# Two-layer hybrid encoder: mLSTM convolution without zero columns, and full-height rows of the running maximum

## Chip, cores and metric

The kernel runs on one core of one Trainium2 chip. The metric is the device time of one execution in microseconds; of a kernel several executions are timed and the median is taken. Lower is better.

## What is computed

The reference is an encoder of two layers over 256 tokens of width 1024, all in float32. A layer normalises `x`, multiplies it by one wide matrix, and hands the parts to four branches: A, a bidirectional mLSTM of 4 heads; B, grouped-query attention with rotary position codes; C, neighbourhood attention; D, differential attention. Each branch's result is projected up and gated, their sum goes through an output projection, and a SwiGLU feed-forward follows. The change touches branch A, of which this is the core:

```python
def centred_dwconv(x, w):
    k = w.shape[0]
    p = k // 2
    s = x.shape[1]
    xp = jnp.pad(x, ((0, 0), (p, p), (0, 0)))
    return sum(xp[:, j:j + s, :] * w[j] for j in range(k))

qk = jax.nn.silu(centred_dwconv(jnp.concatenate([q, k], axis=-1), conv_w))
...
dmat = jnp.where(lower, bt[..., :, None] - bt[..., None, :] + it[..., None, :], -jnp.inf)
inter = bt + m[..., None]
mt = jnp.maximum(inter, dmat.max(-1))
```

The convolution has three taps over tokens, with a zero beyond each end. `mt` is a running maximum per token, head and direction, by which the exponentials are stabilised.

## The kernel before

The weights stream from HBM in halves of 128x1024. ScalarE rounds each half (`whi`), VectorE takes the rest (`wlo`), and TensorE forms every dense product in three passes over these parts into PSUM banks `pd`. Units of weights follow each other in the order of `PLAN` (L38): per layer the inputs of D, B and A, then gates and up-projections between the other branches' inputs, then the output projection and the feed-forward.

The branches' own work is put between the dense products. Each piece is a generator that issues some instructions and yields. Between two runs of dense products (six matmuls as a rule) the program has a slot (`slot`, L296). There `step` (L281) lets each piece advance once if the planner believes that what the piece issued last is through. For this, `Meter` (L140) adds up an estimated cost of each instruction per engine, and all instructions pass through it, which is why nearly every row of the profile shows line 166. On POOL it reckons 0.3 + 0.165 n us for a power of n elements and 0.1 + 0.0021 n us for anything else (L152, 153). A piece's due time is the latest end, on VectorE, ScalarE and POOL, of the engines on which it has just issued something, plus 0.2 us; a step that issued nothing on these three is due at once:

```python
before = [e.until for e in (V, A, G)]
try:
    next(t)
    ready[t] = max([e.until + LAT for e, u in zip((V, A, G), before) if e.until != u] or [0.0])
```

The order so made is fixed at build time; on the chip each engine works through its own queue in that order and waits for semaphores.

`a_head` (L603 to 702) is the piece for one mLSTM head. It takes three tiles `w` (`xp`, `cv`, `th`), transposes the head's q and k on TensorE into a `pa` bank (L613), and has POOL write zeros into the first and last column of each half of `xp` (L617, 618). Next step: ScalarE copies the bank into the columns between (L620) and writes the centre tap's product into `cv` (L625). Next: VectorE adds the outer taps, four instructions of 256 columns (L628 to 630). Then ScalarE's tanh (L632), VectorE's product with 1 + tanh (L634), and on TensorE the scores, `cv` by `cv` in float32 (L640 to 642, `pa<-w` in the profile), and the running maximum (L643 to 647): a matmul by a column of `identr`, a unit matrix, broadcasts one row of `mrow` over 128 partitions, for two directions and the two parts of the number. `mrow` (L213) and `identr` (L201) have 36 partitions; `a_gates` (L518) writes `mrow` once per layer. Two heads are in flight at a time (`fly`).

Beside head 2 and 3, `b_main` (L951) does the rotary codes of branch B on POOL: a power of 20 elements (L974), then for each token tile the products of the keys (`ktok`) and of the queries (`k` tiles of the profile, 512 columns). POOL executes in order.

Of the kernel before, what the change touches and what calls it, by code (L numbers as in the profile page):

```python
# [11 lines left out]
F32 = mybir.dt.float32  # L12
F32R = mybir.dt.float32r
# [6 lines left out]
S = 256  # L20
# [6 lines left out]
# scheduling: how far the engines may be queued ahead of the tensor engine, how early a piece may advance, what a  # L27
# result takes to reach another engine
FILL, TOL, LAT = 2.5, 0.1, 0.2

# column offsets inside w_in
# [10 lines left out]
# offsets inside the per-layer parameter tile  # L42
# [5 lines left out]
# per-feature columns: norm1 gain, norm2 gain, convolution taps  # L48
# [3 lines left out]
# offsets inside the constant tile  # L52
# [4 lines left out]
def unit_order():  # L57
    """Weight units of one layer in the order in which the tensor engine uses them."""
    o = []
    for n in PLAN:  # L60
        if n == "bkv":
            o += [("bkv", 0, 0), ("bkv", 1, 0)]
        elif n[0] == "u":
            o += [("up", n[1], int(n[2]))]
        else:
            o += [("in", n, 0), ("in", n, 1)]
    for kh in (0, 1):
        for c in (0, 1):
            o += [("wo", kh, c)]
    for j in range(NFB):  # L70
        o += [("gu", j, 0), ("gu", j, 1)]
        if 1 <= j < NFB - 1:
            o += [("dn", j - 1, 0)]
    o += [("dn", NFB - 2, 0), ("dn", NFB - 1, 0)]
    return o
# [5 lines left out]
class Res:  # L81
    """Free list over persistent tiles."""
# [20 lines left out]
class Track:  # L103
    """Estimates of when the regions of tiles are written and read by what was emitted so far; it only orders the program."""
# [15 lines left out]
    def after(self, who, reads, writes):  # L120
        """Earliest start of an instruction of `who` by the regions it touches."""
        t = 0.0
        for aps, wr in ((reads, False), (writes, True)):
            for ap in aps:
                name, lo, hi = self.region(ap)
                for l, h, w, e, end in self.acc.get(name, ()):
                    if l < hi and lo < h and (w or wr or name[0:2] in ("pa", "pd")) and e is not who:
                        t = max(t, end + self.HOP)
        return t
# [10 lines left out]
class Meter:  # L140
    """Passes instructions on to an engine and keeps an estimate of when it is through with them."""
# [29 lines left out]
def trunk(ctx: ExitStack, tc, x_in, wts, par, parc, cst, dist, t2w, fg, out):  # L171
# [29 lines left out]
    identr = sb("identr", [36, 128], F32R)  # L201
# [11 lines left out]
    mrow = sb("mrow", [36, 2, S], F32R)  # L213
# [15 lines left out]
    with tc.manual_schedule():  # L229
# [24 lines left out]
        def halves(h):  # L254
            """The first piece is split in two steps, so that the tensor engine can begin after one of them."""
            return (slice(0, 512), slice(512, 1024)) if h == 0 else (slice(0, width(h)),)
# [24 lines left out]
        def step(lst, forced):  # L281
            """Each piece advances once what it issued last is through, as far as the engines have room."""
            for t in list(lst):
                if not forced:
                    if lst is tasks and max(V.until, A.until) > T.until + FILL:
                        return
                    if ready.get(t, 0.0) > T.until + TOL:
                        continue
# [4 lines that stand above are left out]
                except StopIteration:  # L293
                    lst.remove(t)

        def slot(forced=False):  # L296
            """Everything that goes between two runs of dense products; forced: between no products, for what they need."""
# [6 lines left out]
            # at the start the activations come before the weights that follow  # L304
# [13 lines left out]
        def after(eng, t, d=LAT):  # L318
            """Starts a piece once the engine is through."""
            ready[t] = eng.until + d  # L320
            urgent.append(t)

        def later(f, d=1):
            """Runs f after d more slots."""
            pending.append((d, f))

        def until(cond):
            """Advances everything else until the condition holds."""
# [12 lines left out]
        class Unit:  # L341
            """One weight unit [128, 2048], kept as two halves."""
# [28 lines left out]
        def blk512(units, lhs, nkt, done):  # L371
            """[256 tokens, 512] product over the units; the last unit runs one token tile after the other."""
# [60 lines left out]
        G.memset(iz, 0.0)  # L433
        G.memset(va[:, :, :, 128:129], 1.0)

        def tables():
            yield
            yield
            A.activation(identr, ident[0:36, :], AF.Copy)
# [9 lines left out]
        def boundary_chunk(t, c, gcol, st):  # L449
            """Transposes columns [512c, 512c+512) of token tile t into xT and adds to the sums of squares."""  # L450
# [37 lines left out]
        def yt_ok(b):  # L488
            """A branch takes a tile only if one is left for each branch that comes before it."""
# [28 lines left out]
        def a_gates(res):  # L518
            """Gate pre-activations -> a and threshold per token (columns), M as rows (split)."""
# [48 lines left out]
            # w1 rows: [a | B]; w2, w0 rows: zero-padded buffers of the running maximum  # L568
# [16 lines left out]
            A.activation(mrow[:, 0, :], m, AF.Copy)  # L585
            yield
            A.activation(br, br, AF.Exp, scale=-1.0)
            sub_lo(mrow[:, 1, :], m, mrow[:, 0, :])
# [14 lines left out]
        def a_head(B, h, pc):  # L603
            """Short convolution of q and k, then both directions of one head."""
# [11 lines left out]
            xv_ = xp[:, :516].rearrange("p (i n) -> p i n", i=2)  # L616
            G.memset(xv_[:, :, 0:1], 0.0)  # L617
            G.memset(xv_[:, :, 257:258], 0.0)
            yield
            A.activation(xv_[:, :, 1:257], p.rearrange("p (i n) -> p i n", i=2), AF.Copy)  # L620
# [7 lines left out]
            for i in (0, 1):  # L628
                V.scalar_tensor_tensor(cs_[i], xv_[:, i, 0:256], taps[i][0], cs_[i], op0=ALU.mult, op1=ALU.add)
                V.scalar_tensor_tensor(cs_[i], xv_[:, i, 2:258], taps[i][2], cs_[i], op0=ALU.mult, op1=ALU.add)  # L630
# [12 lines left out]
            for d in (0, 1):  # L643
                r = 32 * d + h
                for n in (0, 1):
                    T.matmul(pM[:, d * 256:(d + 1) * 256], identr[0:36, r:r + 1].to_broadcast([36, 128]),
# [90 lines left out]
        def soft_item(B, i, kind):  # L737
            """Two score rows (two heads, or the two components of a head) against all queries."""
            # the scores of D come divided by the head's slope, a power of two: the distances are then added as they are
# [107 lines left out]
        def soft_tail(B, i, c, e):  # L847
            """Normalised weights of one head [2 x 128 queries, 256 keys] -> transposed output rows."""
# [16 lines left out]
            # columns [high part | low part] of the values against the high part of the weights, then the high part  # L865
            # of the values against the low part of the weights
# [28 lines left out]
        def pair_src(B):  # L895
            """Blocks [q 2 pairs | k 2 pairs] in token layout; a block is free after its second pair."""
# [54 lines left out]
        def b_main(B):  # L951
# [12 lines left out]
            # sums of squares per head: 8 query heads then 2 key heads, per token tile  # L964
# [76 lines left out]
        def warm(n):  # L1041
            """Keeps the tensor engine's clock up until the first operands are there."""
# [20 lines left out]
        for l in range(L):  # L1063
# [7 lines left out]
            def tok_evac(B, key, tl=None, halves=False, early=False):  # L1071
# [9 lines left out]
                def done(t, p):  # L1081
                    if halves:
                        if B is Bd:
                            # queries of two heads, times 4 ** (head + 1) / 8
# [19 lines left out]
            def bkv_block():  # L1104
                """Keys and values of B and the gates of A."""
# [25 lines left out]
            def split_v(o, p, t):  # L1131
                """Scaled values, per head [high part | low part]."""
# [92 lines left out]
            # output projection  # L1225
# [28 lines left out]
            # feed-forward  # L1254
# [77 lines left out]
            def final_piece(t, o, n, p):  # L1332
                """Residual and final norm of columns [o, o + n); the last piece of a token tile sends it out."""
# [21 lines left out]
            def last_block():  # L1355
                """The last quarter in two narrow pieces, so that little is left to do after the last product."""
# [12 lines left out]
            # the first half waits longer for the last block's activations, the second ends one token tile after the other  # L1369
# [22 lines left out]
def _layout(inp):  # L1392
    """Host-side layout only: reordering, gathering by static indices, broadcasting of rows."""
    f = {k: np.asarray(v) for k, v in inp.items()}
    # rotary pairs of a head are brought next to each other: [row x1 | col x1 | row x2 | col x2]
# [54 lines left out]
    # neighbourhood bias: entry [p, slot, kc] of a query at column p%64 in row p//64 of its tile  # L1450
# [9 lines left out]
def _consts():  # L1460
    """Tables that depend on shapes alone."""
# [39 lines left out]
```

## Time and profile before

| | |
|---|---|
| runs of the kernel | 1111.65 to 1112.48 us, median 1112.28 us (3 runs) |
| profiled execution | span 1109.9 us from the first to the last instruction, 14766 instructions; the page lists no total beside the span |
| TensorE matmuls (PE) | busy 1086.8 us, 5272 instructions |
| VectorE (DVE) | busy 767.6 us |
| ScalarE (ACT) | busy 616.5 us |
| POOL | busy 156.8 us |
| mean granted clock of TensorE | 0.991 |
| DMA | 184.80 MB, mean 167 GB/s |

Times are in microseconds from the start of the span. A busy time tells how long an engine had an instruction in work; for TensorE, whose matmuls overlap, a busy time near the span doesn't mean that it runs at its peak. Idle time of an engine is put down to what released it. The granted clock is given as a share of 2.4 GHz, so 0.50 is 1.2 GHz. `out<-in` names tiles without their numbers: `w` stands for all of the eight general tiles, `pa` for the five PSUM banks of the pieces, `pd` for the three of the dense products.

### The profile page before, as it was taken

Reading aid. Unit: us, or ns where it says so; the run is one execution under the profiler, and the core shown is the slowest. Engines: PE = TensorE matmul, PEld = TensorE weight load, DVE = VectorE, ACT = ScalarE, POOL = GpSimd, SP = SyncE. Lnnn points to the kernel's source line nnn. Section 1 sums busy time; section 2 is a strip of 40 time slices with the busy share of each in tenths; the row PEclk is TensorE's granted clock in tenths of the full one; section 3 lists DMA queues with packets and bytes.
Section 4 is the critical chain, followed back from the end, with each engine's and each line's share of the span. In section 5 each row is a group of like instructions: output and inputs, shape, how many; then the busy total and the mean of one; then the engine's idle time right before and its main releaser. Section 6 shows DMA issues by size and latency. Waiting matters only on the chain.

```text
span 1109.9 us, 14766 instructions
## 1 busy us (share of the span) xinstructions
PE 1086.8 (98%) x5272; PEld 882.2 (79%) x5272; DVE 767.6 (69%) x1361; ACT 616.5 (56%) x1095; POOL 156.8 (14%) x145
## 2 busy tenths in 40 slices
PE   9999989999999999999999999999999999999997
PEld 7887867888888888888788887778888888888885
DVE  6689779889555755564576978798875666555554
ACT  7665547685444644444467656486853555444443
POOL 0001335054210000000000006152423000000000
PEclk9999989999999999999999999899999999999999
DMA  8444434445555555645544443344456445565551
GB/s 287 153 156 158 148 101 143 154 153 165 193 174 169 190 191 173 204 164 180 187 157 146 159 152 133 115 161 158 140 187 199 162 166 192 184 198 170 190 179 67
DMA packets 52329, 184.80 MB, mean 167 GB/s; under 512 B 6049, under 2 KB 6433, under 8 KB 52257
## 3 DMA queue, kind: packets, MB, share of 16 engines
q1 hardware_dynamic: 50112, 178.57, 48.3%
q10 hardware_dynamic: 2144, 5.31, 1.5%
q8 instruction: 41, 0.67, 0.3%
q14 instruction: 32, 0.25, 0.1%
HBM read 182.80 MB, written 1.05 MB: 166 GB/s over the span
## 4 chain that ended last, share of the span: by engine, by line
PE 77%; issue 13%; DVE 4%; POOL 3%; DMA 1%; ACT 1%; ACTq 0%; POOLq 0%; DVEq 0%
PE pd L166 55%; PE pa L166 22%; DVE sm L166 1%; DVE wlo L166 1%; DVE w L166 1%; DMA x<-in_x_dram 1%; POOL bsm L166 1%; POOL w L166 1%; POOL ktok L166 1%; DVE k L166 1%; DMA raw<-in_wts_dram 0%; POOL sm L166 0%; ACT w L166 0%; DVE rq L166 0%; ACT yt L166 0%
## 5 line engine op out<-in xcount | busy, mean ns | idle before, releaser
L166 PE MATMUL pd<-whi,xT 128*128 128x512 f32 (+1 forms) x1984 | 645.0, 396 | 0.0
L166 DVE TENSOR_TENSOR wlo<-raw,whi 128x1024 fp32r<-128x1024 f32 (+2 forms) x341 | 421.3, 1247 | 106.6 <-ACT whi L166 105.6
L166 PEld LDWEIGHTS pd<-whi,xT 128*128 128x128 f32 x1984 | 371.4, 188 | 86.7
L166 ACT ACTIVATE whi<-raw 128x1024 fp32r<-128x1024 f32 (+2 forms) x341 | 353.7, 1047 | 142.9 <-PE pd L166 91.3
L166 PE MATMUL pd<-wlo,xT 128*128 128x512 f32 (+1 forms) x992 | 387.5, 391 | 0.0
L166 PEld LDWEIGHTS pd<-wlo,xT 128*128 128x128 f32 x992 | 186.5, 188 | 39.4 <-DVE wlo L166 0.3
L166 PE MATMUL pa<-whi,yt 128*128 128x512 f32 x408 | 138.7, 402 | 1.4 <-ACT yt L166 1.4
L166 PEld LDWEIGHTS pa<-whi,yt 128*128 128x128 f32 x408 | 76.6, 188 | 19.7 <-ACT yt L166 1.8
L166 PE MATMUL pd<-whi,yt 128*128 128x512 f32 (+1 forms) x272 | 90.7, 402 | 0.0
L166 PE MATMUL pa<-wlo,yt 128*128 128x512 f32 x204 | 80.6, 395 | 0.0
L166 DVE SCALAR_TENSOR_TENSOR w<-w,pd 128x256 f32<-128x256 f32 x44 | 18.5, 421 | 88.3 <-ACT w L166 88.1
L166 POOL TENSOR_TENSOR st<-st,mhalf 128x2 f32<-128x2 f32 (+1 forms) x6 | 3.9, 656 | 521.6 <-DVE st L166 521.6
L166 ACT ACTIVATE k<-pd,st 128x512 f32<-128x512 f32 (+1 forms) x52 | 31.5, 623 | 56.0 <-PE pd L166 56.0
L166 PEld LDWEIGHTS pd<-whi,yt 128*128 128x128 f32 x272 | 52.4, 194 | 11.9 <-issue 0.4
L166 ACT ACTIVATE w<-pd,st 128x256 f32<-128x256 f32 (+1 forms) x48 | 23.7, 493 | 55.1 <-PE pd L166 52.7
L166 PE MATMUL pd<-wlo,yt 128*128 128x512 f32 (+1 forms) x136 | 54.2, 398 | 0.0
L166 ACT ACTIVATE yt<-pa 128x512 fp32r<-128x512 f32 x34 | 20.3, 598 | 56.2 <-PE pa L166 56.2
L166 PEld LDWEIGHTS pa<-wlo,yt 128*128 128x128 f32 x204 | 38.4, 188 | 8.0
L166 POOL TENSOR_TENSOR acc<-acc,k 128x512 f32<-128x512 f32 x16 | 33.0, 2061 | 80.2 <-DVE k L166 80.2
L166 POOL TENSOR_TENSOR w<-w,sm 128x512 f32<-128x512 f32 x32 | 39.4, 1254 | 21.9 <-DVE sm L166 21.9
L166 ACT ACTIVATE w<-pa 64x256 f32<-64x256 f32 (+3 forms) x66 | 26.7, 409 | 26.7 <-PE pa L166 12.7
L166 DVE TENSOR_TENSOR yt<-pa,yt 128x512 fp32r<-128x512 f32 x30 | 20.7, 689 | 29.1 <-ACT yt L166 29.1
(153 smaller groups left out, 1019.0 us busy)
## 6 DMA issues: line engine op xcount, KB each, us to landing
raw<-in_wts_dram SPq DMA_DIRECT2D x332, 512.0 KB, 3.7
t<-in_t2w_dram ACTq DMA_DIRECT2D x8, 384.0 KB, 3.3
raw<-in_wts_dram SPq DMA_DIRECT2D x8, 272.0 KB, 2.9
pt<-in_par_dram SPq DMA_DIRECT2D x1, 584.0 KB, 7.0
pt<-in_par_dram ACTq DMA_DIRECT2D x1, 584.0 KB, 3.6
out_dram<-k SPq DMA_DIRECT2D x2, 288.0 KB, 2.1
x<-in_x_dram ACTq DMA_DIRECT2D x1, 512.0 KB, 9.7
k<-in_fg_dram ACTq DMA_DIRECT2D x1, 512.0 KB, 3.5
```

The lines of the kernel that those rows point to most:

```text
L166: return f(out, *a, **k)
```

## The change

Three edits. The zero columns and their memsets go: `xp` holds 2 x 256 columns without a gap, and the outer taps leave out the column that would have read a zero. `mrow` and `identr` get 128 partitions, so that the broadcast matmuls contract over 128 rows; the rows beyond 36 of `mrow` are zeroed once at the start. Comments are taken out all over the file, which the program doesn't see and which is left out here.

```diff
-    identr = sb("identr", [36, 128], F32R)
+    identr = sb("identr", [128, 36], F32R)
...
-    mrow = sb("mrow", [36, 2, S], F32R)
+    mrow = sb("mrow", [128, 2, S], F32R)
...
         G.memset(iz, 0.0)
+        G.memset(mrow.bitcast(F32), 0.0)
...
-            A.activation(identr, ident[0:36, :], AF.Copy)
+            A.activation(identr, ident[:, 0:36], AF.Copy)
...
-            A.activation(mrow[:, 0, :], m, AF.Copy)
+            A.activation(mrow[0:36, 0, :], m, AF.Copy)
...
-            sub_lo(mrow[:, 1, :], m, mrow[:, 0, :])
+            sub_lo(mrow[0:36, 1, :], m, mrow[0:36, 0, :])
...
-            xv_ = xp[:, :516].rearrange("p (i n) -> p i n", i=2)
-            G.memset(xv_[:, :, 0:1], 0.0)
-            G.memset(xv_[:, :, 257:258], 0.0)
-            yield
-            A.activation(xv_[:, :, 1:257], p.rearrange("p (i n) -> p i n", i=2), AF.Copy)
+            xv_ = xp[:, :512].rearrange("p (i n) -> p i n", i=2)
+            yield
+            A.activation(xp[:, :512], p, AF.Copy)
...
             for i in (0, 1):
-                V.scalar_tensor_tensor(cs_[i], xv_[:, i, 0:256], taps[i][0], cs_[i], op0=ALU.mult, op1=ALU.add)
-                V.scalar_tensor_tensor(cs_[i], xv_[:, i, 2:258], taps[i][2], cs_[i], op0=ALU.mult, op1=ALU.add)
+                V.scalar_tensor_tensor(cs_[i][:, 1:256], xv_[:, i, 0:255], taps[i][0], cs_[i][:, 1:256],
+                                       op0=ALU.mult, op1=ALU.add)
+                V.scalar_tensor_tensor(cs_[i][:, 0:255], xv_[:, i, 1:256], taps[i][2], cs_[i][:, 0:255],
+                                       op0=ALU.mult, op1=ALU.add)
...
-                    T.matmul(pM[:, d * 256:(d + 1) * 256], identr[0:36, r:r + 1].to_broadcast([36, 128]),
+                    T.matmul(pM[:, d * 256:(d + 1) * 256], identr[:, r:r + 1].to_broadcast([128, 128]),
                              mrow[:, n, :], start=n == 0, stop=n == 1)
```

## Rows read from the trace of the kernel before

**Rows 1.** The page, part 1: busy us (share of the span) x instructions.

```profile
PE 1086.8 (98%) x5272; PEld 882.2 (79%) x5272; DVE 767.6 (69%) x1361; ACT 616.5 (56%) x1095; POOL 156.8 (14%) x145
```

**Rows 2.** Waits of TensorE: us in total, times, longest us.

```profile
PE pa L166 <- DVE w L166: 9.9, 2, 5.0
PE pa L166 <- DVE rq L166: 1.9, 2, 0.9
```

**Rows 3.** Windows: length, busy us (x instructions) of each engine, PEclk, DMA share, GB/s.

```profile
60.00:146.80 86.80, 84.56 (x413) 67.91 (x411) 74.02 (x169) 52.64 (x98) 21.85 (x29) 1.00 0.45 148
147.00:157.00 10.00, 7.47 (x18) 5.55 (x19) 7.71 (x18) 2.80 (x5) 1.85 (x2) 0.50 0.31 105
157.10:696.30 539.20, 532.79 (x2603) 432.54 (x2601) 375.81 (x658) 303.94 (x538) 77.54 (x67) 1.00 0.51 167
696.50:703.00 6.50, 6.50 (x16) 4.77 (x17) 4.23 (x12) 1.23 (x2) 0.00 (x0) 0.50 0.24 81
```

**Rows 4.** Timeline of TensorE, both layers: start us, us, what, idle before it.

```profile
149.53 2.07 PE L166 MATMUL pa<-w 128*128 128x256 f32 x4 [4.96 <-DVE w L166]
...
696.45 2.08 PE L166 MATMUL pa<-w 128*128 128x256 f32 x4 [4.95 <-DVE w L166]
```

**Rows 5.** Timeline of POOL, ScalarE and VectorE ahead of the first layer's wait.

```profile
128.64 4.44 POOL L166 TENSOR_TENSOR bsm<-bsm,mhalf 128x20 f32<-128x20 f32 x1 [22.15 <-DVE bsm L166]
...
139.23 0.14 POOL L166 MEMSET w<- 128x2 f32 x2
...
139.40 0.60 ACT L166 ACTIVATE w<-pa 128x512 f32<-128x512 f32 x1 [3.57 <-POOL w L166]
...
140.47 4.33 DVE L166 SCALAR_TENSOR_TENSOR w<-w,pc,w 128x256 f32<-128x256 f32 x4 [2.92 <-ACT w L166]
...
140.83 2.79 POOL L166 TENSOR_TENSOR k<-k,w 128x512 f32<-128x512 f32 x2
...
144.72 1.75 DVE L166 TENSOR_TENSOR wlo<-raw,whi 128x1024 fp32r<-128x1024 f32 x1
...
147.80 1.67 DVE L166 SCALAR_TENSOR_TENSOR w<-w,w 128x512 f32<-128x512 f32 x1
```

**Rows 6.** The same timeline, 134 to 138 us, TensorE, ScalarE and VectorE.

```profile
134.23 0.60 PE L166 MATMUL pa<-ident,acc 128*128 128x128 f32 x4
...
134.78 1.05 ACT L166 ACTIVATE whi<-raw 128x1024 fp32r<-128x1024 f32 x1
...
135.27 1.14 DVE L166 TENSOR_TENSOR w<-w,pa 128x256 f32<-128x256 f32 x4
...
136.33 1.21 DVE L166 TENSOR_TENSOR wlo<-raw,whi 128x1024 fp32r<-128x1024 f32 x1
```

**Rows 7.** The chain of waits: start us, us, what; one run of six dense matmuls.

```profile
165.27 1.40 PE pd L166 x6
```

**Rows 8.** Timeline: head 2's convolution, and POOL's products of `ktok`.

```profile
125.35 1.98 DVE L166 SCALAR_TENSOR_TENSOR w<-w,pc,w 128x256 f32<-128x256 f32 x4
...
136.11 1.62 POOL L166 TENSOR_TENSOR w<-ktok,w 128x64 f32<-128x64 f32 x2
```

**Rows 9.** Timeline of TensorE: the `mrow` block, and a block of full height.

```profile
132.06 0.73 PE L166 MATMUL pa<-mrow,identr 36*128 36x256 f32 x4
132.72 0.51 PE L166 MATMUL pd<-whi,xT 128*128 128x512 f32 x1
...
132.06 0.53 PEld L166 LDWEIGHTS pa<-mrow,identr 36*128 36x128 f32 x4 [0.33 <-issue]
...
189.21 0.63 PE L166 MATMUL pa<-re,vb 128*128 128x256 f32 x4
189.68 1.04 PE L166 MATMUL pa<-ident,k 128*128 128x128 f32 x8
```

**Rows 10.** Groups of POOL by form: busy us, mean ns, idle before.

```profile
L166 POOL MEMSET w<- 36x512 f32 x4 | 2.0, 519 | 67.2 <-ACT w L166 34.8 <-PE pd L166 32.5
```

**Rows 11.** Timeline of ScalarE: head 1's copy.

```profile
89.28 0.60 ACT L166 ACTIVATE w<-pa 128x512 f32<-128x512 f32 x1 [0.74 <-POOL w L166]
```

## The prediction

> **What bounds the kernel now.** I read the busy shares first. TensorE is busy for 1086.8 of 1109.9 us [rows 1], so only two things can shorten the program: less matmul time, or the few stretches in which TensorE stands still or runs slowly. The waits of TensorE name the stretches in which it stands: in the whole trace it waits 9.9 us for VectorE's `w` tiles, in 2 waits of up to 5.0 us, and little else [rows 2]. The windows show those in which it is slow: between 60 and 703 us the granted clock is 1.00 except in two stretches, 147 to 157 and 696.5 to 703 us, where it is 0.50, that is 1.2 instead of 2.4 GHz [rows 3]. The timeline shows that both belong together: TensorE idles 4.96 us before the `pa<-w` matmuls at 149.53 and 4.95 us before those at 696.45, and the slow clock covers each wait's end and what follows [rows 4]. It is the same place in both layers: the score matmul (L641) of head 3 of the mLSTM branch, with dense products queued behind it.
>
> Followed backwards [rows 5]: the matmul needs `cv`, finished by VectorE's 1.67 us instruction at 147.80 (L634); that needs the tanh (L632), that the convolution (4.33 us from 140.47, L628 to 630), and that ScalarE's copy at 139.40 (L620), which stood 3.57 us, by the trace for POOL's `w`. POOL's two memsets of zero columns (L617, 618) run at 139.23. They need nothing that late; they stand in POOL's queue behind the rotary work of branch B, which begins with a power of 4.44 us at 128.64 on which the planner reckons 0.3 + 0.165 x 20 = 3.6 us. So a write of two columns puts off a chain that TensorE waits for. From the timeline alone the copy could have run when the transposes (0.60 us from 134.23) were through, near 134.9; in ScalarE's queue a `whi` split stands there until 135.83 [rows 6].
>
> **The memsets (removed).** The stalls cost 4.96 + 4.95 = 9.9 us idle. At half clock TensorE was busy 7.47 us in one stretch and 6.50 us in the other [rows 3], which at full clock take half: 7.0 us lost. Together 16.9 us are to be had. How much of it comes back hangs on the new chain. Copy: without the memsets the first step of `a_head` writes on no engine but TensorE, so its `ready` is 0 and the copy is emitted at the next slot instead of after the planner's estimate for POOL. I take that as one slot (six dense matmuls, 1.40 us [rows 7]), which puts the copy ahead of that `whi`: copy and the two centre taps 134.9 to 136.3. Convolution: VectorE is then through its four products (1.14 us from 135.27), so it can start at 136.4, ahead of the `wlo` of 136.33 [rows 6]. Its length is open. Head 2's took 1.98 us while POOL was idle; head 3's 4.33 us, beside POOL's `k` products of 1.4 us each [rows 5, 8]. At 136.4 POOL does the small products of the `ktok` part, two in 1.62 us [rows 8]. Bounds 1.98 and 4.33 us; I take 3.2, the middle, since POOL is busy but with shorter work. Then VectorE makes that `wlo` (1.21 us [rows 6], beside POOL 1.75 [rows 5]) while ScalarE does the tanh, and then L634, 1.67 us beside POOL, less than half of that if the convolution's ratio holds for it. With 1.2 for each: 136.4 + 3.2 + 1.2 + 1.2 = 142.0; at the bounds 136.4 + 1.98 + 1.21 + 0.76 = 140.3 and 136.4 + 4.33 + 1.75 + 1.67 = 144.2.
>
> The Trainium skill (SBUF — State Buffer, section "SBUF: two separate sides") has a rule that speaks against this move: a VectorE instruction with two SBUF inputs and a POOL instruction that reads SBUF lock each other out for a whole instruction. The trace agrees in kind (1.98 against 4.33 us); by the rule each of the four instructions could lose one `ktok` product, some 2 us (an estimate), and end inside the bounds above.
>
> When does TensorE ask? It arrived at 149.53 - 4.96 = 144.57; every later step of the piece moves one slot up too, so now at about 143.2. Against 142.0 that is no wait, at the worst bound 1.0 us. An idle time of 0.9 us (the `rq` waits, rows 2) lies in the stretch from 157 to 696 us, whose clock is 1.00 [rows 3], so a rest of that size costs no clock. I put 0.5 us per layer, 1.0 in all, with 0 and 2.0 as ends.
>
> **Late next.** The stall let the other engines catch up; without it TensorE comes some 8 us (16.9 / 2) sooner to what follows. VectorE has the 2.92 us before the convolution, where it idled [rows 5], and the split weights due then come earlier than now. I add nothing beyond the 1.0 us.
>
> **The full-height rows.** Eight times (4 heads, 2 layers) four matmuls multiply 36 rows of `mrow` by a broadcast column. The block takes 132.72 - 132.06 = 0.66 us, and its first weight load waits 0.33 us of "issue", so it doesn't lie under the matmul before it [rows 9]. The nearest block of four full-height matmuls of 256 columns takes 189.68 - 189.21 = 0.47 us [rows 9]. Hence 0.19 us saved if the new block behaves like that row, and up to 0.33 more for the entry; 0 if the height means nothing. A loss I exclude: the columns streamed are the same. Between 0 and 0.52 us I take 0.25, nearer to 0.19 because the matmul before the block still streams during part of the 0.33: 8 x 0.25 = 2.0 us, ends 0 and 4.2.
>
> By the Trainium skill (TensorEngine Tiling (Array Packing), section "Key Properties") a change of tiling mode drains TensorE; the 0.33 us at the entry agree, and by that rule alone the sum would lose the whole of it, 8 x 0.52 = 4.2 us instead of 2.0 (an estimate).
>
> **The rest.** The outer taps are one column shorter of 256 (1 ns each) and the copy writes the same 512 columns: nothing. `identr` holds 36 columns instead of 128: one ScalarE instruction at the start, nothing. A memset of `mrow` is added, 128x512, against 0.52 us for a 36x512 one [rows 10]; POOL runs it in the first 2 us and has no other work until the first norm, and `mrow` is first read beyond 100 us: nothing; uncovered it would cost about that 0.5 us once. Head 1's copy also waits for POOL, 0.74 us [rows 11], without a wait of TensorE behind it (its matmul waits for the gates): nothing. It moves up by about two slots, and with it some 2 us of VectorE work; TensorE waits for VectorE nowhere near it (the two waits on `w` are head 3's), so nothing again. No DMA is added or moved. Comments are removed too.
>
> **Sum.** 1109.9 - 16.9 + 1.0 - 2.0 = 1092.0 us of span. The page gives no total of the profiled execution beside its span; the median of the runs, 1112.28, is 2.4 us above it, and I keep these 2.4: **1094.4 us**, 1.6% less. Own range: 1112.3 - 16.9 - 4.2 = 1091.2 to 1112.3 - 16.9 + 2.0 + 0 = 1097.4.
>
> **Rivals.**
>
> *A shorter wait that still drops the clock.* If the convolution and L634 keep their durations of now and VectorE's order lets nothing be gained but the 3.57 us of the copy, while TensorE asks one slot earlier, 4.96 - 3.57 + 1.40 = 2.8 us of idle time stay per layer. For it: POOL works on until 149 either way. The clock was still 1.00 up to 146.8 us, 2.2 us into the first wait [rows 3], and then fell, so the 7.0 us of slow clock stay: 1112.3 - 16.9 - 2.0 + 2 x 2.8 + 7.0 = 1106.0. Against it: VectorE stood idle for 2.92 us before the convolution, and the shift moves it out of the `k` products.
>
> *The wait is not the memsets'.* The copy's release could hang on the tile's former reader, so that it stays at 139.4, and only the height of the rows counts: 1110.3, or 1112.3 if that gives nothing. Against it: the copy starts 0.17 us after the memsets do.
>
> *Slower: asked for sooner, ready no sooner.* If POOL's port holds the convolution until the same 144.8 as now, wherever it starts, while the planner, which knows of no such hold, emits L641 one slot sooner, each stall grows by 1.40 us; the slow clock follows it. With nothing from the height, 1112.3 + 2.8 + 0.5 (the second stretch of slow clock grown to the first's, half of 7.47 - 6.50) = 1115.6. It decides from the point at which the convolution ends after 144.8; against it stands that 8.4 us pass from 136.4 to there, for work of 1.98.
>
> **How the numbers follow.** Forecast 0.73 (1091.2 to 1097.4), shorter wait 0.13 (1106.0), not the memsets' 0.08 (1110.3 to 1112.3), slower 0.06 (1115.6). The range takes in the first two: 1091 to 1106, 0.86 of the chance. A measurement of this kernel tells 0.2% (2.2 us, 1110.1 to 1114.5) from no change; so faster 0.86, same 0.08, slower 0.06.
>
> **What the changed profile would show.** Right: no `w<- 128x2` memset on POOL; TensorE's waits for VectorE's `w` down from 9.9 to under 2 us; granted clock 1.00 from 60 to 690 us; head 3's convolution some 3 to 4 us earlier relative to POOL's power; the `mrow` matmuls as 128*128, a block near 0.5 us, without the 0.33 us of "issue". Wrong: a wait over 2 us before a `pa<-w`, or a new one within the 30 us behind it (`wlo`, `rq`), with the clock at 0.50 after it; or the copy still waiting for POOL.

## The result and the profile after

The changed kernel takes 1093.42 us (median of 4 runs, 1091.94 to 1093.63), the kernel before on the same chip 1111.99 (4 runs, 1111.65 to 1112.48): 18.6 us or 1.7% less, ratio 0.9832 with an interval of 0.9818 to 0.9846. The forecast was 1094.4. The profiled execution took 1093.29 us, its span is 1091.5 us against 1109.9 before, so 1.8 us lie around it.

The page of the changed kernel, part 1:

```profile
PE 1077.9 (99%) x5272; PEld 879.6 (81%) x5272; DVE 765.2 (70%) x1361; ACT 616.8 (57%) x1095; POOL 156.6 (14%) x130
```

Beside [rows 1], POOL has 15 instructions fewer: 16 memsets gone (8 heads with 2 each), one of `mrow` added. All other engines issue as many as before. TensorE is busy 8.9 us less, though its 5272 matmuls are the same in number: it ran at half clock for less time, and 32 of them are of another height.

The waits of TensorE (us in total, times, longest us), to be read beside [rows 2]:

```profile
PE pa L166 <- DVE rq L166: 3.0, 2, 1.5
...
PE pa L166 <- DMA x<-in_x_dram: 1.0, 1, 1.0
```

The line for VectorE's `w`, 9.9 us before, is gone. The one for `rq` has grown from 1.9 to 3.0.

The timeline of the changed kernel, first layer, head 3 (start us, us, what, idle before it), beside [rows 5]:

```profile
126.36 4.46 POOL L166 TENSOR_TENSOR bsm<-bsm,mhalf 128x20 f32<-128x20 f32 x1 [20.40 <-DVE bsm L166]
...
132.09 0.58 ACT L166 ACTIVATE w<-pa 128x512 f32<-128x512 f32 x1
...
133.64 2.23 DVE L166 SCALAR_TENSOR_TENSOR w<-w,pc,w 128x255 f32<-128x255 f32 x4
...
133.96 1.02 POOL L166 TENSOR_TENSOR w<-ktok,w 128x64 f32<-128x64 f32 x2
...
135.79 1.48 DVE L166 TENSOR_TENSOR wlo<-raw,whi 128x1024 fp32r<-128x1024 f32 x1
...
137.19 0.88 DVE L166 SCALAR_TENSOR_TENSOR w<-w,w 128x512 f32<-128x512 f32 x1
...
140.05 1.02 PE L166 MATMUL pa<-w 128*128 128x256 f32 x4
```

The two traces are shifted against each other, so times are counted from the start of POOL's power. ScalarE's copy came at 10.8 us, now at 5.7, with no wait in its brackets; the convolution began at 11.8, now at 7.3; L634 ended at 20.8, now at 11.7. TensorE was ready for the scores at 15.9 (144.57) and stood until 20.9; now it takes them up at 13.7, when they have been there for 2.0 us (138.07 against 140.05).

The `mrow` block of head 2 in TensorE's timeline, changed kernel, beside [rows 9]:

```profile
128.53 1.02 PE L166 MATMUL pa<-w 128*128 128x256 f32 x4
129.21 0.83 PE L166 MATMUL pa<-mrow,identr 128*128 128x256 f32 x4
129.87 0.39 PE L166 MATMUL pd<-whi,xT 128*128 128x512 f32 x1
130.10 0.40 PE L166 MATMUL pd<-wlo,xT 128*128 128x512 f32 x1
...
129.18 0.64 PEld L166 LDWEIGHTS pa<-mrow,identr 128*128 128x128 f32 x4
```

The weight load no longer waits 0.33 us for "issue". The block itself takes 129.87 - 129.21 = 0.66 us, as long as with 36 rows; what is saved lies at its two ends. From the first score matmul to the second dense one it is 130.10 - 128.53 = 1.57 us, where the kernel before, and the one with 64 rows below, take 1.95: 0.38 us per head, 8 x 0.38 = 3.0 us.

The wait that has grown stands 30 us further on. The timeline of the changed kernel, and under it that of the kernel before at the same work:

```profile
164.20 0.97 PE L166 MATMUL pa<-kb,rq 64*128 64x256 f32 x12
...
165.58 1.83 DVE L166 TENSOR_SCALAR k<-k,mvt,sm 128x128 f32<-128x128 f32 x4
...
168.10 0.50 PE L166 MATMUL pa<-kb,rq 64*128 64x256 f32 x4
...
169.62 0.41 DVE L166 TENSOR_TENSOR rq<-pa,rq 128x256 fp32r<-128x256 f32 x1
...
170.08 0.74 PE L166 MATMUL pa<-kb,rq 64*128 64x256 f32 x8 [1.48 <-DVE rq L166]
```

```profile
177.60 0.98 PE L166 MATMUL pa<-kb,rq 64*128 64x256 f32 x12
...
178.44 1.83 DVE L166 TENSOR_SCALAR k<-k,mvt,sm 128x128 f32<-128x128 f32 x4
...
181.50 0.51 PE L166 MATMUL pa<-kb,rq 64*128 64x256 f32 x4
...
182.47 0.41 DVE L166 TENSOR_TENSOR rq<-pa,rq 128x256 fp32r<-128x256 f32 x1
...
182.94 0.74 PE L166 MATMUL pa<-kb,rq 64*128 64x256 f32 x8 [0.93 <-DVE rq L166]
```

In both, VectorE scales the mLSTM branch's result (`k<-k,mvt,sm`) ahead of an attention item's `rq`, and takes the same 4.0 us from the one to the other (165.58 to 169.62, 178.44 to 182.47). TensorE's own work in this stretch is the same as well: 3.90 us from its twelve matmuls to its four (164.20 to 168.10, 177.60 to 181.50). What has moved is the one engine against the other: the four matmuls came 3.06 us behind the scaling and now come 2.52, so TensorE is 0.54 us further ahead of VectorE, and that is the growth of the wait from 0.93 to 1.48. And the wait costs more than itself. The windows of the changed kernel (length, busy us of each engine, granted clock, DMA share, GB/s), first layer, then the same place in the second:

```profile
60.00:170.00 110.00, 108.61 (x559) 88.22 (x557) 98.98 (x234) 68.18 (x138) 31.89 (x29) 1.00 0.44 149
170.00:175.00 5.00, 4.92 (x26) 4.09 (x27) 4.93 (x9) 5.00 (x15) 2.04 (x2) 0.66 0.30 105
...
707.00:710.00 3.00, 1.52 (x17) 1.18 (x16) 2.96 (x7) 2.52 (x9) 1.37 (x2) 1.00 0.06 23
```

In layer 1 the clock falls to 0.50 for part of the five microseconds after the wait: 5.0 x (1 - 0.66) = 1.7 us lost. In layer 2 TensorE stands as long (busy 1.52 of 3 us) and the clock stays at 1.00.

So the span's 18.4 us are: 9.9 us of waits for `w`; 7.0 - 1.7 = 5.3 us of slow clock; 3.0 us of height; less 1.1 us of longer waits for `rq`, and 0.3 us less wait for a DMA. Together 17.4; 1.0 us stays unassigned.

### The profile page after: what moved, and what is told of

Same layout as the page of the kernel before. It is cut to its first block, busy times and chain, and to the rows that moved or that the text cites. A ratio compares the mean times of both kernels' runs of the same rounds, so it can differ in the third digit from the quotient of the medians.

```text
span 1091.5 us, 14727 instructions
## 1 busy us (share of the span) xinstructions
PE 1077.9 (99%) x5272; PEld 879.6 (81%) x5272; DVE 765.2 (70%) x1361; ACT 616.8 (57%) x1095; POOL 156.6 (14%) x130
## 4 chain that ended last, share of the span: by engine, by line
PE 95%; DVE 3%; DMA 1%; issue 0%; ACT 0%; POOLq 0%; POOL 0%; ACTq 0%
PE pd L166 69%; PE pa L166 26%; DVE sm L166 1%; DVE wlo L166 1%; DVE k L166 1%; DMA x<-in_x_dram 1%; DVE rq L166 0%; DVE acc L166 0%; ACT yt L166 0%; DVE mvt L166 0%; ACT pa L166 0%; DVE x L166 0%; ACT k L166 0%; POOLq L1499 0%; POOL st L166 0%
## 5 line engine op out<-in xcount | busy, mean ns | idle before, releaser
L166 DVE TENSOR_TENSOR wlo<-raw,whi 128x1024 fp32r<-128x1024 f32 (+2 forms) x341 | 426.5, 1263 | 113.5 <-ACT whi L166 112.9
L166 PE MATMUL pd<-whi,yt 128*128 128x512 f32 (+1 forms) x272 | 87.1, 390 | 0.0
L166 POOL TENSOR_TENSOR acc<-acc,k 128x512 f32<-128x512 f32 x16 | 30.5, 1907 | 85.0 <-DVE k L166 85.0
L166 ACT ACTIVATE w<-w,sm 128x256 f32<-128x256 f32 x64 | 31.7, 501 | 11.0 <-DVE sm L166 6.3
```

The source lines that it names most:

```text
L166: return f(out, *a, **k)
```

## The experiments

Theory: POOL's two memsets, standing in POOL's queue, held a chain that TensorE waits for, and wait and clock came from that; the height of the rows counts by itself. Rivals: that the planner's new order brings the gain, not the missing wait; that the extra columns cost VectorE; that TensorE asks sooner for what is ready no sooner. The first four kernels were timed against nine runs of the kernel before with a median of 1110.89 us (1110.09 to 1111.74), the last four, on another chip, against nine with 1111.93 (1110.07 to 1112.78).

**E1, the height alone.** The kernel before with the full-height tile:

```
-    identr = sb("identr", [36, 128], F32R)
+    identr = sb("identr", [128, 36], F32R)
-    mrow = sb("mrow", [36, 2, S], F32R)
+    mrow = sb("mrow", [128, 2, S], F32R)
+        G.memset(mrow.bitcast(F32), 0.0)
...
-    T.matmul(pM[...], identr[0:36, r:r + 1].to_broadcast([36, 128]),
+    T.matmul(pM[...], identr[:, r:r + 1].to_broadcast([128, 128]),
```

> The kernel before with only the full-height rows (mrow and identr of 128 partitions); zero columns and their memsets on POOL stay. Theory (the memsets' wait made the two stalls, the height is a gain of its own): the two waits of 4.9 us for VectorE's w and the 0.50 clock behind them stay, the eight mrow blocks save 0.38 us each, 3 us: ratio to before 0.997, some 1109 us. Rival 1 (the height matters only by the 0.33 us at the entry): 8 x 0.33 = 2.6 us at most, and the matmul behind the block stays slow (0.34 us to the next). Rival 2 (the height has a share in the stalls): under 1105 us.

Measured: 1105.84 us (1104.87 to 1106.62), ratio 0.9956 (0.9942 to 0.9969). That is 5.0 us, more than the height was to give, and between the expected 1109 and the 1105 of the second rival. Apart from the memsets, the instructions of VectorE, ScalarE, POOL and TensorE's matmuls stand in the order of the kernel before, and the stall is still there; waits and timeline of E1:

```profile
PE pa L166 <- DVE w L166: 10.5, 2, 5.2
```

```profile
137.83 0.60 ACT L166 ACTIVATE w<-pa 128x512 f32<-128x512 f32 x1 [3.65 <-POOL w L166]
...
147.97 2.08 PE L166 MATMUL pa<-w 128*128 128x256 f32 x4 [5.25 <-DVE w L166]
```

These are [rows 4, 5] with a shift of some 1.5 us. What differs is how long the clock stays low; windows of E1:

```profile
146.00:160.00 14.00, 12.03 (x53) 10.13 (x54) 11.64 (x27) 5.37 (x9) 1.29 (x2) 0.77 0.32 110
680.00:706.00 26.00, 20.79 (x102) 17.23 (x101) 19.96 (x36) 11.45 (x23) 10.80 (x14) 0.93 0.35 112
```

A mean clock of 0.77 over 14 us is 6.4 us at half, 0.93 over 26 us is 3.6: 10 us, where [rows 3] have 10.0 + 6.5. So 3.0 us belong to the height (8 x 0.38, as above), and in this run most of the rest to shorter stretches of slow clock after the same stall; why they are shorter is not settled. But the profiled run is the fastest of the five, 1104.87 us with a mean granted clock of 0.995 over the span. The other four have 0.992, hardly more than the 0.991 or 0.992 of the nine runs of the kernel before, and take 1105.60 to 1106.62 us. So what gives the median of E1 its other 2 us stays open.

**E2, the convolution alone.** The change without the height (the edits of E1 undone in the changed kernel).

> The change without the full-height rows: the convolution without zero columns alone. Theory: the two stalls before head 3's scores go, the new waits for rq stay; 3 us above the whole change: 1096 to 1097 us, ratio to before 0.986. Rival (both parts are needed together): above 1100 us.

Measured: 1095.00 us (1094.70 to 1095.26), ratio 0.9856 (0.9843 to 0.9870), 1 us under the range expected. TensorE has no wait for `w`, the convolution takes 2.20 us from 134.79, and TensorE takes up the scores at 141.23. The entry to the block is back, by the timeline of TensorE's weight loads in E2:

```profile
130.29 0.53 PEld L166 LDWEIGHTS pa<-mrow,identr 36*128 36x128 f32 x4 [0.33 <-issue]
```

So the convolution part alone gives 15.9 us, where the whole change gave 18.6. E1's 5.0 and E2's 15.9 add up to 2.3 us more than the whole change; the 2 us of E1 that are open above are in this sum. A shorter slow clock is worth nothing once there is none, which would explain it, but that isn't shown.

**E3, the old order without the wait.** In the changed kernel the planner still reckons with two memsets that are not emitted, so that every engine's instructions stand in the order of the kernel before:

```
+            for _ in (0, 1):
+                G.until = max(G.until, track.after(G, [], [xp[:, :512]])) + 0.1042
+                track.note(G, [], [xp[:, :512]], G.until)
             A.activation(xp[:, :512], p, AF.Copy)
```

> The whole change, but the planner goes on counting the two memsets per head on POOL, which are not issued: the instructions of every engine stand in the order of the kernel before, and only the wait is gone. Theory (the wait is what costs): no wait over 0.5 us before head 3's scores, 1093 to 1097 us. Rival (the new order is what pays, the earlier place of the copy above all): the copy may run earlier, but behind the whi split, and a wait of 1 us or more stays before the scores; near 1100 us or more.

Measured: 1093.06 us (1092.68 to 1093.42), ratio 0.9839 (0.9826 to 0.9852). Waits of TensorE in E3, and its timeline:

```profile
PE pa L166 <- DVE rq L166: 2.0, 2, 1.0
PE pa L166 <- DVE w L166: 1.8, 2, 0.9
```

```profile
142.52 1.71 DVE L166 SCALAR_TENSOR_TENSOR w<-w,w 128x512 f32<-128x512 f32 x1
...
144.29 1.13 PE L166 MATMUL pa<-w 128*128 128x256 f32 x4 [0.90 <-DVE w L166]
```

Compared instruction by instruction, E3's trace has the order of the kernel before on VectorE, ScalarE, POOL and in TensorE's matmuls. The old order with the wait away is as fast as the change, so the gain is the wait's and not the order's. One thing was missed: 0.90 us of wait for `w` stay per layer, since the chain runs one slot later here than in the changed kernel and L634 takes 1.71 us where it takes 0.88 there. In exchange the waits for `rq` stay near their length of before, 2.0 us in the two layers.

**E4, the new order with the wait.** E1 with its memsets emitted past the planner, so that it reckons as in the changed kernel, and POOL still runs them:

```
-            G.memset(xv_[:, :, 0:1], 0.0)
-            G.memset(xv_[:, :, 257:258], 0.0)
+            nc.gpsimd.memset(xv_[:, :, 0:1], 0.0)
+            nc.gpsimd.memset(xv_[:, :, 257:258], 0.0)
```

> Full-height rows, zero columns and memsets kept, but the planner doesn't count the memsets: every engine's order is that of the changed kernel, and ScalarE's copy still waits for POOL. Theory: POOL comes to the memsets some 10.6 us after its power begins (before: 128.64 to 139.23), while TensorE now asks one slot sooner, so head 3's scores wait longer than before, 6 to 7 us per layer with the 0.50 clock behind it; slower than e1_height_only, 1111 to 1116 us. Rival (the order pays, not the wait): 1094 to 1100 us.

Measured: 1105.57 us (1104.55 to 1107.46), ratio 0.9953 (0.9941 to 0.9966): the time of E1, not a slower one. Timeline of E4:

```profile
126.35 4.44 POOL L166 TENSOR_TENSOR bsm<-bsm,mhalf 128x20 f32<-128x20 f32 x1 [19.33 <-DVE bsm L166]
...
133.89 0.60 POOL L166 TENSOR_TENSOR w<-ktok,w 128x64 f32<-128x64 f32 x2
...
136.01 0.10 POOL L619 MEMSET w<- 128x2 f32 x1
...
136.15 0.60 ACT L166 ACTIVATE w<-pa 128x512 f32<-128x512 f32 x1 [4.04 <-POOL w L619]
...
137.21 4.30 DVE L166 SCALAR_TENSOR_TENSOR w<-w,pc,w 128x256 f32<-128x256 f32 x4 [3.56 <-ACT w L166]
...
144.91 1.58 PE L166 MATMUL pa<-w 128*128 128x256 f32 x4 [4.76 <-DVE w L166]
```

The expectation of 1111 to 1116 us was wrong, and the trace shows why. TensorE does ask sooner, 13.8 us behind the power where it was 15.9. But the scores are ready sooner by as much, 18.6 us behind the power where it was 20.9, so the stall is 4.76 us and not 1.4 us more than 4.96. Two things bring this. The memsets come 9.6 us behind the power instead of 10.6: POOL's pair of `ktok` products takes 0.60 us here, while VectorE waits, and took 1.62 [rows 8] beside VectorE's `wlo` [rows 6]. And from the start of the convolution to the scores it is 7.7 us (137.21 to 144.91) instead of 9.1 [rows 4, 5], as VectorE's new order puts L634 ahead of three small `sm` rows (1.5 us) that stood before it. So with the wait left in, the new order brings nothing over E1. The waits for `rq` are 2.8 us in E4, near the 3.0 of the changed kernel, against 2.0 in E3: their growth belongs to the order, not to the stall that went.

**E5, the columns kept, on another queue.** E1 with the zero columns written by VectorE:

```
-            G.memset(xv_[:, :, 0:1], 0.0)
-            G.memset(xv_[:, :, 257:258], 0.0)
+            V.memset(xv_[:, :, 0:1], 0.0)
+            V.memset(xv_[:, :, 257:258], 0.0)
```

> Full-height rows; the zero columns stay, but VectorE writes them instead of POOL (16 instructions more on VectorE, some 0.1 us each). Theory (what cost was POOL's queue, not the columns): the 4.9 us waits go, ratio to before 0.984 to 0.989, 1093 to 1099 us. Rival (the columns or the two instructions ahead of the copy cost, on whatever engine): a wait of 2 us or more before head 3's scores, 1103 us or more.

Measured: 1091.73 us (1091.51 to 1092.32), ratio 0.9821 (0.9808 to 0.9835), with the changed kernel at 1091.63 in the same comparison (E8). Timeline of E5:

```profile
134.06 0.07 DVE L166 MEMSET w<- 128x2 f32 x2
...
143.12 1.13 PE L166 MATMUL pa<-w 128*128 128x256 f32 x4 [0.27 <-DVE w L166]
```

That is less than the 1093 to 1099 expected. Two memsets of 0.07 us together, on VectorE, give the whole gain without taking a column away. So neither the columns nor the taps' last column counted, only the queue that the memsets stood in.

**E6, 64 rows in place of 128.** In the changed kernel:

```
-    mrow = sb("mrow", [128, 2, S], F32R)
+    mrow = sb("mrow", [64, 2, S], F32R)
...
-    identr[:, r:r + 1].to_broadcast([128, 128])
+    identr[0:64, r:r + 1].to_broadcast([64, 128])
```

> The whole change, but mrow and the slice of identr have 64 partitions instead of 128. Theory (any height below 128 is another tiling of the array, and the switch costs): the mrow blocks are as slow as with 36 rows, 0.33 us of issue before each and 0.34 us to the second matmul behind; as e2_conv_only, 2 to 3 us above the whole change, 1095 to 1096 us. Rival (it was the odd 36 rows): as the whole change, 1092 to 1094 us.

Measured: 1095.83 us (1094.85 to 1097.92), ratio 0.9860 (0.9846 to 0.9873), 4.2 us above E8. TensorE's timeline in E6:

```profile
129.26 1.02 PE L166 MATMUL pa<-w 128*128 128x256 f32 x4
130.21 0.53 PEld L166 LDWEIGHTS pa<-mrow,identr 64*128 64x128 f32 x4 [0.33 <-issue]
130.21 0.73 PE L166 MATMUL pa<-mrow,identr 64*128 64x256 f32 x4
...
131.21 0.39 PE L166 MATMUL pd<-wlo,xT 128*128 128x512 f32 x1
```

131.21 - 129.26 = 1.95 us, the same as with 36 rows: of the three heights only the full one is free of the step, and it isn't paid by the row. Of the 4.2 us this is 3.0. The profiled runs of E6 and E8, whose spans lie 4.9 us apart (1094.6 and 1089.7), show what the rest can be: in E6 the clock fell behind the second layer's wait for `rq` (1.47 us, ending at 710.27), which costs 5.0 x (1 - 0.66) = 1.7 us, and in E8 it didn't. The window of E6:

```profile
710.00:715.00 5.00, 4.73 (x24) 3.91 (x25) 4.93 (x9) 5.00 (x17) 2.04 (x2) 0.66 0.33 107
```

**E7, the scaling later.** The changed kernel, with the scaling of the mLSTM result put behind the wait for the gate, which it does not need but its reader does:

```
             yield
             yield
+            while "go" not in B:
+                yield
             for t in (0, 1):
                 for h in range(4):
                     ...
             SM.put(rs)
-            while "go" not in B:
-                yield
```

> The whole change, and the mLSTM branch's normalisation (eight VectorE instructions per layer, 1.1 and 1.8 us for four) waits until the output gate of the branch is there, some 100 us later, instead of standing in the stretch in which TensorE now waits 1.5 us for rq. Theory (VectorE's load in that stretch is what is late next): both rq waits under 0.5 us, clock 1.00 throughout, 3 to 4.5 us below the whole change, 1088.5 to 1091 us. Rival (the wait hangs on the chain of branch B's scores on ScalarE and POOL): the rq waits stay at 1 us or more, 1092 us or more.

Measured: 1088.08 us (5 runs, 1087.74 to 1088.21), ratio 0.9787 (0.9774 to 0.9800), 3.6 us below E8, a little faster than was expected of it. Waits of TensorE in E7, complete, and two rows of its timeline:

```profile
PE pd L166 <- POOL ident masks.py:199: 1.5, 1, 1.5
PE pa L166 <- ACT yt L166: 1.4, 2, 0.7
PE pa L166 <- DMA x<-in_x_dram: 0.7, 1, 0.7
```

```profile
167.40 0.41 DVE L166 TENSOR_TENSOR rq<-pa,rq 128x256 fp32r<-128x256 f32 x1
...
168.03 0.97 PE L166 MATMUL pa<-kb,rq 64*128 64x256 f32 x12
```

`rq` is made 2.2 us sooner than in the changed kernel and TensorE doesn't wait for it in either layer; its granted clock is 1.00 from 60 to 1075 us, with TensorE busy 1013.63 of those 1015 us. So the waits for `rq` come from the scaling that stands ahead of it. In the kernel before VectorE has the same rows in the same order ahead of `rq`, so the same is likely there; no run shows it. E7 beats both kernels.

**E8, the changed kernel again,** in the same comparison as E5 to E7.

> The whole change, unaltered, as the measure for the other three of this call: 1092 to 1094 us; ratio to before 0.983 to 0.985.

Measured: 1091.63 us (1091.47 to 1092.72), ratio 0.9822 (0.9808 to 0.9835). Waits and windows of E8:

```profile
PE pa L166 <- DVE rq L166: 3.0, 2, 1.5
```

```profile
146.00:190.00 44.00, 42.52 (x252) 34.77 (x251) 39.00 (x78) 31.38 (x74) 17.44 (x12) 1.00 0.46 150
680.00:740.00 60.00, 58.51 (x330) 47.97 (x329) 51.18 (x100) 43.52 (x95) 20.39 (x15) 1.00 0.46 153
```

The same two waits of 1.5 us, and no fall of the clock in either layer. Its span is 1089.7 us, 1.8 us below the first profile's 1091.5, and the slow stretch there was worth 1.7. That agrees with the spread of the changed kernel's runs, 1091.5 to 1093.6 us, being this stretch's coming or not. Only profiled runs show the stretch itself, but the mean clock over the span goes the same way in all eight runs: 0.997 in those of 1093.29, 1093.55 and 1093.63 us and in E8's slowest (1092.72), 0.998 or 0.999 in those of 1091.47 to 1091.94.

## Why the prediction was right

**The memsets, held.** That POOL's queue and not the columns held the chain is shown from three sides: without memsets (E2), with the old order and no wait (E3), and with the memsets on VectorE (E5) the stall goes; with the new order and the wait (E4) it stays. Of the signs that the prediction named, three were not met to the letter: the clock was not 1.00 throughout, the convolution came 4.5 us earlier and not 3 to 4, and the `mrow` block takes 0.66 us and not some 0.5. Of the 16.9 us that were to be had, 9.9 us of idle time came back whole and 5.3 of the 7.0 us of slow clock in the profiled run, all 7.0 where the clock held, as in E8. The 1.0 us put in as a rest did not arise: the chain was ready 2.0 us ahead of TensorE, where the sum had it ready 143.2 - 142.0 = 1.2 us ahead.

**The length of the convolution, mis-sized on the safe side.** The middle of 1.98 and 4.33, 3.2 us, was taken, and it took 2.23; `wlo` 1.48 for 1.2, L634 0.88 for 1.2. Beside POOL's short products (a pair in 1.02 us) VectorE lost 0.25 us; the 4.33 us were beside `k` products of 1.4 us each. The Trainium skill (SBUF — State Buffer, section "SBUF: two separate sides") would have each of the two engines lock the other out for a whole instruction. The trace agrees in kind: POOL's pair took 1.02 us beside the convolution and 0.60 us earlier (at 130.79) without it. It doesn't agree in size for VectorE, which lost 0.25 us where the prediction's estimate was some 2; by [rows 8], with 0.81 us for one product, that estimate would have been 4 x 0.81 = 3.2 us and its end outside the bounds.

**The slot, a little more than one.** TensorE came to the scores 13.7 us behind the power, not 15.9: 2.2 us sooner, where one slot of 1.40 was taken. The chain had moved up by 9, so nothing hung on it.

**The height, too small: 3.0 us, not 2.0.** The step that failed is the value per head. The nearest full-height block was taken as the model for the inside of the block (0.66 to 0.47 us), and most of the 0.33 us at the entry was given away, since the matmul before it might still stream. It was the other way about: the inside stayed at 0.66 us, and the whole of the 0.38 us lies at entry and exit (0.27 and 0.11, by the rows of E6 against those of the changed kernel). The Trainium skill (TensorEngine Tiling (Array Packing), section "Key Properties") says that TensorE drains when the tiling mode changes; E6 agrees, as 64 rows pay the same 0.33 us of "issue" as 36, and the sum by that rule alone, 4.2 us, was too large by the inside of the block, which the rule does not speak of.

**"Late next: I add nothing", wrong by 1.1 us, and by 1.7 more where the clock fell.** The prediction looked at the split weights and at VectorE's work around the convolution, and took the `rq` waits of [rows 2] as a given. It moved only the chain and left the order further on as it was; the planner, reckoning without memsets, placed that anew too, and TensorE came 0.54 us sooner, as seen from VectorE, to a wait that was already there. E3 (2.0 us) and E4 (2.8 us) show that the order does this. The prediction's list of wrong signs had it (`rq`, within 30 us, with the clock at 0.50 after it); its sum did not. E7 shows what the wait hangs on and takes it away.

**What lies around the span.** 2.4 us were kept from the median of before; the changed kernel's profiled run has 1.8. Every run whose time and span are both on record lies 1.7 to 1.9 us above its span, so the 2.4 had set the median of the runs against the span of a faster one. The height (1.0 us), the rest (1.0) and this offset (0.6) made the forecast too slow, `rq` and the clock behind it (1.1 and 1.7) too fast. That 1094.4 lies 1.0 us from 1093.4 is in part luck: the terms are further off than their sum.

**The rivals.** "A shorter wait" and "asked for sooner" would both have shown a wait before `pa<-w`; there is none. The slower one needed a convolution that ends as late as before; it ends 9.5 us behind the power (133.64 + 2.23), where it was 16.2. E4 asks sooner with the wait left in and was not slower, since the scores were ready sooner too. "Not the memsets'" falls with E5. That E1 and E4 end at 1105.8 and 1105.6, where the shorter wait was priced at 1106.0, is chance: their waits are as long as ever.

## What to carry to other kernels

A write of two columns costs next to nothing by its duration and here some 16 us by its queue (E2): look at what stands ahead of a helper's instruction on its in-order engine, and put it on an engine that is through in time, before taking the work away. When a planner's inputs change, it also places anew what lies further on: take the waits that the old trace already shows, and ask for each who stands ahead of it on its engine; here moving that work gave another 3.6 us. Where one small matmul block of less than full height stands between full ones, price the step in and out of it, not the block.

## What was not expected of the hardware

The profiled runs with the changed kernel's order (the changed kernel, E2, E4, E6, E8) have ten waits of TensorE for `rq` of 1.40 to 1.49 us. Behind two of them, of 1.48 us in the first profile and 1.47 us in E6, the granted clock fell to 0.50, for a loss of 1.7 us each; behind the other eight it stayed at 1.00, in the other layers of the same two runs too. The eight waits of 0.93 to 1.02 us in the kernel before, E1, E3 and E5 left it at 1.00. After the six stalls of 4.7 us or more it always fell, but for 16.5 us in all in the kernel before, some 10 in E1 and some 7 in E4. What decides this is open: no run here varied the length of a wait by itself.

A block of 64 rows pays what one of 36 pays (0.33 us of "issue" at the entry, 1.95 us from the scores to the second dense matmul), and at full height the four matmuls of the block are no faster than before, 0.66 us.
